# Output projection of a decoder block: 8 x 8 products of tiles, or seven products of quarters

## The chip, the cores and the metric

The kernel runs on one core of one Trainium2 chip. The metric is the device time of one execution in microseconds (us); lower is better. Engines: PE (TensorE, matrix products; PEld is its weight load), DVE (VectorE), ACT (ScalarE), POOL (GpSimd) and SP (SyncE). SP and POOL here mostly issue DMA transfers. Each engine works through its own queue of instructions in a fixed order and waits for semaphores of the others. "Lnnn" is a line of the kernel file.

## The reference

One decoder block, 1024 tokens by 1024 channels, in float32:

```python
y = (sigmoid(gate_sb + b_gate[0]) * (o_sb @ w_branch_sb)        # first branch: stick-breaking attention
     + sigmoid(gate_gla + b_gate[1]) * (o_gla @ w_branch_gla))  # second branch: gated linear attention
h = x + y @ w_out                                               # the output projection
hn = rms_norm(h, norm_ffn_g)
a, g = split(hn @ w_ffn_in)                                     # 1024 -> 2 x 2816
h = h + (gelu(causal_conv(a) + conv_b) * g) @ w_ffn_out
out = rms_norm(h, norm_final_g)
```

The change concerns `y @ w_out` (1024 x 1024 by 1024 x 1024) and the norm behind it.

## The kernel before

Every large product is made in three matmuls: each float32 operand is split into a high half (a rounded copy of type fp32r, a CAST on ACT at L122) and a low half (operand minus high half, on DVE at L113), and high x high + high x low + low x high are summed in one PSUM bank (128 x 512; there are eight). `split`, and the operand makers `piece`, `cut` and `parts` that call it, thus cost one ACT and one DVE instruction of 128 x 512 for each operand.

The functions are generators, and the code steps them against one another; a scheduler then orders the instructions of each engine by what it expects to be ready, and the engines run in that order. SBUF tiles come in three sizes from pools: `t8` (128 x 2048, 16 of them), `t4` (128 x 1024, 14 of them) and `t2` (128 x 512, 11 of them).

- `branch(b, o, w)` projects a branch: for 16 pairs (channel tile, half of the tokens) 12 matmuls, times the gate. The first branch leaves its product in `yb[th, kh]` (token half, channel half; the channels lie on the partitions), the second adds it and splits the sum into `yq`.
- `project()` makes the output projection in four parts (half of the tokens by half of the columns). In a part, each of four token tiles is 8 x 3 matmuls into one bank, then an add of `x`. After the second part of each token half a row is whole: it is stored to `h_d`, normalized (`norm_rows`: square and root on ACT, reciprocal and scaling on DVE) and later turned on PE into the next product's operand: `turn` for tiles 0 to 3; `turn_sums` for tiles 4 to 7, which also makes some of the sums that the next product needs.
- `fast(jobs, hq, EARLY)` is the product with `w_ffn_in`: 22 jobs by Winograd's form of Strassen, with seven products of quarters each. Two of the seven need only the first token half (`hq["11"]`, `hq["12"]`), and the first six jobs make these two early, while the projection ends: 12 steps "early" with 12 matmuls each. With the loading and preparing steps that makes 58 steps in all.
- `phase(first, ...)` begins the last matrix, `w_ffn_out`, in the same form. Its first operands are made ahead: the loop over the remaining job steps counts `n` and, from `n >= AT_END` (51) on, puts `first(0)` into `ready` (L1444, L1445). `weight_sums` makes sums of quarters of `w_ffn_out`, which `pace(3)` steps from `n > FFN_FROM` (18) on.
- The code between: 14 steps of the projection, one job step, two projection steps, two job steps, one projection step; so three job steps are taken ahead of the loop and 55 are left for it.

Of the kernel before, what the change touches and what calls it, by code (L numbers as in the profile page):

```python
# [17 lines left out]
P = 128  # L18
# [39 lines left out]
AT_END = 51  # L58
HEADS_AT = 2
# [9 lines left out]
def block_kernel(ctx: ExitStack, tc: tile.TileContext, x, norm_mix_g, w_in, b_gate, w_alpha_up, b_alpha,  # L69
# [32 lines left out]
    def dram(name, rows, cols, dt=F32):  # L102
        return dp.tile([rows, cols], dt, tag=name, name=name)
# [67 lines left out]
    wsum_d = dram("wsum_d", NH * P, 2 * D)  # L171
# [898 lines left out]
    yq, yb, hq, hs1 = {}, {}, {}, {}  # L1070

    def branch(b, o, w):
# [11 lines left out]
        for n in range(2 * NK):  # L1084
# [27 lines left out]
    def weight_sums():  # L1112

        def rows(k):
            if k < NH:
                v = t4(), t4()
                for i in range(2):
                    nc.sync.dma_start(v[i], w_ffn_out[(i * NH + k) * P:(i * NH + k + 1) * P, :])
                return v

        nxt = rows(0)
        for k in range(NH):
            (a, b), nxt = nxt, rows(k + 1)
# [48 lines left out]

    def project():

        def raws(dh):
            return [load(w_out[k * P:(k + 2) * P, dh * HALF:(dh + 1) * HALF], 2)[:, n]
                    for k in range(0, NK, 2) for n in range(2)]

        parts = [(0, 0), (0, 1), (1, 1), (1, 0)]
        ws = [flat(piece(r)) for r in raws(0)]  # L1180
        late = []

        def late_turn():
# [6 lines left out]
        for part, (th, dh) in enumerate(parts):  # L1190
            c = slice(dh * HALF, (dh + 1) * HALF)
            second, turned = part % 2, part % 2 == 0
            if not second:
                hr = []
                for i in range(4 * th, 4 * th + 4, 2):
                    v = by(t8(F32), 2)
                    nc.sync.dma_start(v, x[i * P:(i + 2) * P, :].rearrange("(n p) c -> p n c", p=P))
                    hr += [v[:, 0], v[:, 1]]
            else:
                for a in ("22", "s3", "s2") if th else ("11", "12"):  # L1200
                    hq[a] = quarter()
            nws = [] if turned else ws
            for n, i in enumerate(range(4 * th, 4 * th + 4)):
                t = slice(n * P, (n + 1) * P)
                pt = bank()
                for k in range(NK):
                    yh, yl = yq[th, k // 4]
                    wh, wl = ws[k]
                    for m, (a, b) in enumerate(((yh, wh), (yl, wh), (yh, wl))):
                        nc.tensor.matmul(pt, a[:, k % 4, t], b, start=(k == 0 and m == 0),  # L1210
                                         stop=(k == NK - 1 and m == 2))
                    if n == 3 and turned:
                        ws[k] = wh = wl = None
                        if k % 2 == 0:
                            raw = load(w_out[k * P:(k + 2) * P, (HALF - dh * HALF):(D - dh * HALF)], 2)
                        nws.append(flat(piece(raw[:, k % 2])))
                h = hr[n]
                add(h[:, c], pt, h[:, c])
                if second:
                    nc.gpsimd.dma_start(h_d[i * P:(i + 1) * P, :], h)  # L1220
                    hn = t4()
                    norm_rows(h, gf, hn)
                    late.append((hn, i))
                if late and (len(late) > 1 if second else n == 1):
                    late_turn()
                yield
            ws = nws
            if second:
                hr = None
                for kh in range(2):  # L1230
                    del yq[th, kh]
# [248 lines left out]
```

## Time and profile before

| | us |
|---|---|
| median of three runs | 1386.93 (1386.27 to 1387.03) |
| the profiled execution, its own time | 1386.67 |
| its span in the trace | 1384.8 |
| granted TensorE clock | 0.997 |
| projection matmuls (L1210), 384 | 88.8 busy |

The span is that of the one profiled execution, from the first to the last instruction; the rest of its time lies around it. In the groups, a row reads: line, engine, operation, tiles, shape, count, then busy us and mean ns of one, then idle time just before with what ended it. An engine that is busy all the time sets the pace, and a wait elsewhere costs nothing by itself.

### The profile page before, as it was taken

How to read it: one execution, taken by the hardware profiler on the slowest of the kernel's cores; microseconds unless marked ns; L12 is line 12 of the kernel's file. 1: busy time of each engine (PE TensorE's matmuls, PEld its weight loads, DVE VectorE, ACT ScalarE, POOL GpSimd, SP SyncE). 2: the span in 40 equal slices, each digit the busy share in tenths (PEclk: the TensorE clock that was granted, in tenths of full speed). 3: DMA queues.
4: the chain of work that ended last, by engine and by line, in shares of the span. 5: the costliest groups of instructions: out<-in, count | busy, mean ns of one | idle time of the engine just before them, and what ended most of it. 6: DMA issues, size and time to landing. Idle time of an engine off the chain costs nothing.

```text
span 1384.8 us, 18329 instructions
## 1 busy us (share of the span) xinstructions
PE 1372.4 (99%) x6559; PEld 1138.8 (82%) x6559; DVE 1064.6 (77%) x1640; ACT 643.9 (46%) x1244; POOL 136.3 (10%) x233
## 2 busy tenths in 40 slices
PE   9999999999999999999999999999999999999997
PEld 6788888888888888888888788888888888888886
DVE  6388688874878877658348998998888977896765
ACT  7334445653766664724126443343333334454654
POOL 2002123101111002200000000000000000000000
PEclk9999999999999999999999999999999999999999
DMA  6335278448776567673325245554444537953332
GB/s 239 132 117 151 84 221 251 143 158 210 216 158 151 131 197 237 198 237 136 136 91 177 52 120 187 196 189 152 150 163 152 182 107 272 322 163 102 99 101 105
DMA packets 164108, 227.92 MB, mean 165 GB/s; under 512 B 10938, under 2 KB 105276, under 8 KB 163506
## 3 DMA queue, kind: packets, MB, share of 16 engines
q1 hardware_dynamic: 134944, 139.01, 33.0%
q0 software_dynamic: 22496, 73.73, 16.8%
q10 hardware_dynamic: 6578, 14.03, 2.7%
q8 instruction: 51, 0.84, 0.3%
q14 instruction: 39, 0.32, 0.1%
HBM read 160.28 MB, written 66.45 MB: 164 GB/s over the span
## 4 chain that ended last, share of the span: by engine, by line
PE 95%; DVE 3%; ACT 1%; issue 0%; DMA 0%; ACTq 0%; DVEq 0%
PE bank L205 58%; PE bank L1343 15%; PE bank L385 6%; PE bank L1210 6%; PE bank L871 3%; PE bank L828 2%; PE bank L842 2%; DVE t L113 2%; PE bank L494 1%; PE bank L340 1%; DVE t L119 1%; PE bank L562 1%; PE bank L1007 1%; PE bank L970 0%; PE bank L994 0%
## 5 line engine op out<-in xcount | busy, mean ns | idle before, releaser
L205 PE MATMUL bank<-t,t 128*128 128x512 f32 x3624 | 861.1, 393 | 0.9 <-DVE t L113 0.7
L205 PEld LDWEIGHTS bank<-t,t 128*128 128x128 f32 x3624 | 676.5, 188 | 143.1 <-DVE t L113 1.6
L113 DVE TENSOR_TENSOR t<-t,t 128x512 fp32r<-128x512 f32 (+3 forms) x655 | 434.6, 697 | 93.5 <-ACT t L122 87.2
L122 ACT CAST t<-t 128x512 fp32r<-128x512 f32 (+1 forms) x543 | 320.3, 627 | 325.4 <-DVE t L113 81.0
L119 DVE TENSOR_TENSOR t<-bank,t 128x512 f32<-128x512 f32 x266 | 179.3, 685 | 97.9 <-PE bank L205 54.9
L1343 PE MATMUL bank<-t,t 128*128 128x512 f32 x924 | 209.6, 389 | 0.0
L1343 PEld LDWEIGHTS bank<-t,t 128*128 128x128 f32 x924 | 173.5, 188 | 36.0
L113 DVE TENSOR_TENSOR t<-bank,t 128x512 fp32r<-128x512 f32 (+4 forms) x124 | 69.5, 574 | 27.5 <-ACT t L122 26.9
L1210 PE MATMUL bank<-t,t 128*128 128x512 f32 x384 | 88.8, 391 | 0.0
L1241 ACT ACTIVATE t<-t,vcol 128x1024 f32<-128x1024 f32 x22 | 27.4, 1245 | 127.5 <-DVE t L119 127.5
L113 DVE TENSOR_TENSOR t<-t 128x512 f32<-128x512 f32 x120 | 83.3, 701 | 4.1 <-DMA t<-in_w_ffn_in_dram 3.7
L1210 PEld LDWEIGHTS bank<-t,t 128*128 128x128 f32 x384 | 71.6, 188 | 14.6
L119 DVE TENSOR_TENSOR t<-t,t 128x512 f32<-128x512 f32 x115 | 75.5, 686 | 9.8 <-ACT t L628 8.6
L122 ACT CAST t<-bank 128x512 fp32r<-128x512 f32 (+3 forms) x120 | 60.3, 512 | 48.8 <-PE bank L842 26.8
L385 PE MATMUL bank<-t,t 128*128 128x512 f32 x336 | 77.9, 391 | 0.0
L385 PEld LDWEIGHTS bank<-t,t 128*128 128x128 f32 x336 | 62.7, 188 | 13.1 <-DVE t L113 0.2
L1243 DVE SCALAR_TENSOR_TENSOR t<-t,vcol,t 128x1023 f32<-128x1023 f32 (+1 forms) x44 | 56.3, 1279 | 14.1 <-ACT t L1241 13.9
L833 DVE TENSOR_TENSOR_SCAN t<-t,t 128x128 f32<-128x128 f32 (+1 forms) x64 | 51.6, 816 | 17.5 <-ACT t L830 17.2
L828 PE MATMUL bank<-t,t 128*128 128x128 f32 (+3 forms) x192 | 54.6, 369 | 0.0
L842 PE MATMUL bank<-ident,t 128*128 128x128 f32 x288 | 53.2, 273 | 0.0
L871 PE MATMUL bank<-t,t 128*128 128x256 f32 (+1 forms) x320 | 51.0, 276 | 1.2 <-ACT t L122 0.7
L830 ACT ACTIVATE t<-bank 128x128 f32<-128x128 f32 (+3 forms) x96 | 46.9, 507 | 7.2 <-DMA osb_d<-t 3.2
(164 smaller groups left out, 813.5 us busy)
## 6 DMA issues: line engine op xcount, KB each, us to landing
t<-in_w_ffn_in_dram SPq DMA_DIRECT2D x50, 512.0 KB, 5.1
t<-in_w_in_dram SPq DMA_DIRECT2D x43, 512.0 KB, 5.3
act_d<-t POOLq DMA_DIRECT2D x22, 512.0 KB, 5.8
t<-in_w_ffn_out_dram SPq DMA_DIRECT2D x22, 512.0 KB, 7.6
wsum_d<-t POOLq DMA_DIRECT2D x22, 512.0 KB, 4.5
t<-act_d SPq DMA_DIRECT2D x22, 512.0 KB, 5.9
t<-wsum_d SPq DMA_DIRECT2D x44, 256.0 KB, 3.1
t<-in_w_ffn_out_dram SPq DMA_DIRECT2D x33, 256.0 KB, 2.7
```

The lines of the kernel that those rows point to most:

```text
L113: nc.vector.tensor_tensor(out=o, in0=a, in1=b, op=ALU.subtract)
L119: nc.vector.tensor_tensor(out=o, in0=a, in1=b, op=ALU.add)
L122: nc.scalar.copy(h, src)
L205: nc.tensor.matmul(pt, a[:, kk], b[:, kk], start=start and kk == 0 and m == 0, stop=stop and kk == k - 1 and m == 2)
L385: nc.tensor.matmul(pt, a[:, k % 4, t], b, start=k == 0 and m == 0, stop=k == NK - 1 and m == 2)
L828: nc.tensor.matmul(z[:, 0:w], q[:, a, e, ts_], kk[:, e, b0 * P:b1 * P], start=a == 0, stop=a == 1)
L833: nc.vector.tensor_tensor_scan(out=kr, data0=kr, data1=above[:, 0:w], initial=1.0, op0=ALU.mult, op1=ALU.max)
L842: nc.tensor.transpose(pt[:, b * P:(b + 1) * P], ke[:, b * P:(b + 1) * P], ident)
L871: nc.tensor.matmul(po[:, c0:2 * P], vt[b][:, head, :], a[b // 4][:, b % 4, c0:], start=(b == 0 and n == 0), stop=(b == nb - 1 and n == 1))
L1210: nc.tensor.matmul(pt, a[:, k % 4, t], b, start=(k == 0 and m == 0), stop=(k == NK - 1 and m == 2))
L1243: nc.vector.scalar_tensor_tensor(out=cv[:, i:], in0=av[:, :S - i], scalar=col(V_CW, (2 - i) * NF + f), in1=cv[:, i:], op0=ALU.mult, op1=AL ...
L1343: nc.tensor.matmul(pts[m][i], a[:, t], b, start=(k == 0 and x_ == 0), stop=(k == NH - 1 and x_ == 2))
```

## The change

The output projection is made as seven products of quarters (512 x 512 by 512 x 512, four k tiles by four token tiles by three matmuls). The second branch no longer splits its sum; it leaves plain sums in `yb`, from which `project` forms the sums of quarters in place. Sums of the quarters of `w_out` are made by `weight_sums`, stepped beside the second branch, and go through a new DRAM tensor `osum_d`. The products run in the order op1, op2, op5, op6, op3, op7, op4 with operands prepared `LEAD` = 2 ahead. Rows of the result are summed into `x` partly by DVE and partly by DMA transfers that accumulate (`onto`, on POOL's queue). op3 ends tile by tile over its last two k tiles, op4 over all four. The norms of tiles 0 to 3 follow op3, those of tiles 4 to 7 follow op4. The table `AMONG` says how many job steps go ahead of each of the last six projection steps: nine in all, so 49 are left for the loop. `AT_END` and `FFN_FROM` stay as they are.

```diff
+LEAD = 2
+AMONG = 1, 0, 1, 1, 3, 3
...
+    wsum_d, osum_d = dram("wsum_d", NH * P, 2 * D), dram("osum_d", 4 * P, 2 * D)
...
             else:
                 mul(sg, pt, sg)
-                add(sg, sg, y)
-                split(*(a[:, i % 4] for a in yq[th, i // 4]), sg)
+                add(y, sg, y)
...
-    wsteps = weight_sums()
+    wsteps = weight_sums(w_ffn_out, NH, wsum_d)
+    osteps = weight_sums(w_out, 4, osum_d)
...
+    def onto(o, a):
+        nc.gpsimd.dma_start(o, a, accum_op=ALU.add)
...
+        def cut(src):
+            v = t4(F32R)
+            v = v[:, :HALF], v[:, HALF:]
+            split(*v, src)
+            return v
...
+        def op1(k):
+            w = weights(w_out, k, 0)
+            a = cut(yb[0, 0][:, k])
+            sub(yb[0, 0][:, k], yb[0, 0][:, k], yb[1, 0][:, k])
+            return a, cut(w)
...
+        def norm(i):
+            nc.gpsimd.dma_start(h_d[i * P:(i + 1) * P, :], hr[i])
+            hn = t4()
+            norm_rows(hr[i], gf, hn)
+            hr[i] = None
+            late.append((step[0], hn, i))
+
+        def done1(i, pt):
+            nc.scalar.copy(c[:, i], pt)
+
+        def done2(i, pt):
+            add(left(i), pt, left(i))
+            onto(left(i), c[:, i])
+
+        def done5(i, pt):
+            nc.scalar.copy(d[:, i], pt)
+            onto(right(i), d[:, i])
+            onto(right(4 + i), d[:, i])
+
+        def done6(i, pt):
+            add(c[:, i], pt, c[:, i])
+            onto(left(4 + i), c[:, i])
+            onto(right(4 + i), c[:, i])
+            add(right(i), right(i), c[:, i])
+
+        def done3(i, pt):
+            add(right(i), pt, right(i))
+            norm(i)
+
+        def done7(i, pt):
+            add(right(4 + i), pt, right(4 + i))
+            add(left(4 + i), pt, left(4 + i))
+
+        def done4(i, pt):
+            sub(left(4 + i), left(4 + i), pt)
+            norm(4 + i)
...
+            if tail:
+                for i in range(4):
+                    for k in range(4 - tail, 4):
+                        rank(k, i)
+                    done(i, pts[i])
+                    step[0] += 1
+                    if late and late[0][0] + 3 <= step[0]:
+                        turn_late()
+                    yield
...
-    for _ in branch(1, og, w_branch_gla):
+    for n, _ in enumerate(branch(1, og, w_branch_gla)):
+        fill(osteps, n % 2)
         pace(1)
...
-    for _ in islice(steps, 14):
-        pace(2)
-    fill(jobs, 1)
-    fill(steps, 2)
-    fill(jobs, 2)
-    fill(steps, 1)
+    fill(steps, 26)
+    for n in AMONG:
+        fill(jobs, n)
+        fill(steps, 1)
+    fill(steps, 16)
```

Lines of the changed file are shifted: the helpers by 2 (L113 becomes L115, L119 L121, L122 L124, L205 L207), the projection's matmul is L1316, `turn_sums`'s transposes L351, the convolution's lines L1353 (ACT), L1355 (DVE) and L1357 (ACT). In the rows below a bracket names what a row waits for: an engine, or a transfer issued on SP or ACT (DMAHW) or on POOL (DMASW).

**First place, PE, the end of the projection.** Before, the transposes of token tile 6 (`t4_1328`) stand behind all 24 matmuls of tile 7 (the last bank is 7067):

```order
L1210 MATMUL bank_1337_7067<-t4_1302_6896,t8_1206_6264 128x512
L1210 MATMUL bank_1337_7067<-t4_1302_6896,t8_1205_6263 128x512
L349 MATMUL bank_1342_7102<-ident_66,t4_1328_7035 128x128 [waits DVE_49]
L349 MATMUL bank_1342_7102<-ident_66,t4_1328_7035 128x128 x3
L349 MATMUL bank_1343_7103<-ident_66,t4_1328_7035 128x128 x4
```

Now op4's banks 7083, 7084 and 7085 are tiles 4, 5 and 6, 7156 is the first early product of job 0, and `t4_1368` is the normalized tile 4:

```order
L1316 MATMUL bank_1358_7083<-t4_1367_7100,t4_1366_7097 128x512 [waits DVE_49]
L1316 MATMUL bank_1358_7083<-t4_1367_7100,t4_1366_7097 128x512
L1316 MATMUL bank_1359_7084<-t4_1367_7100,t4_1366_7097 128x512 x2
L207 MATMUL bank_1380_7156<-t8_1324_6908,t4_1356_7077 128x512
L207 MATMUL bank_1380_7156<-t8_1323_6907,t4_1356_7077 128x512
L1316 MATMUL bank_1360_7085<-t4_1364_7092,t4_1363_7089 128x512 x2
L1316 MATMUL bank_1360_7085<-t4_1367_7100,t4_1366_7097 128x512 x3
L351 MATMUL bank_1391_7198<-ident_66,t4_1368_7117 128x128 [waits DVE_49]
L351 MATMUL bank_1391_7198<-ident_66,t4_1368_7117 128x128 x3
```

Between tile 4's last matmul and its transposes stand nine matmuls.

**Second place, DVE, ahead of the first full job.** `t4_1392` (before) and `t4_1450` (now) are the low half of that job's first piece. Before:

```order
L113 TENSOR_TENSOR t2_1390_7395<-t8_1389_7392 128x512 [waits DMAHW2_49,DMAHW1_49]
L119 TENSOR_TENSOR t4_1383_7334<-bank_1385_7349,t4_1383_7334 128x512 [waits PE_49,Activation_49]
L113 TENSOR_TENSOR t2_1391_7396<-t8_1389_7392,t2_1390_7395 128x512 [waits DVE_49]
L113 TENSOR_TENSOR t2_1393_7402<-t8_1389_7392 128x512
L113 TENSOR_TENSOR t2_1394_7403<-t8_1389_7392,t2_1391_7396 128x512 [waits DVE_49]
L113 TENSOR_TENSOR t2_1405_7466<-t8_1398_7415 128x512 [waits DMAHW5_49,DMAHW3_49]
L113 TENSOR_TENSOR t2_1406_7467<-t8_1398_7415,t2_1405_7466 128x512 [waits DVE_49]
L113 TENSOR_TENSOR t4_1392_7399<-t2_1391_7396,t4_1392_7399 128x512 [waits Activation_49]
```

Now (`t8_1440`, `t8_1442` and `t2_1433` belong to the sums of `last_sums`; bank 7515 is the last early product):

```order
L115 TENSOR_TENSOR t8_1442_7467<-t2_1405_7270,t8_1441_7466 128x4x128 [waits Activation_49]
L115 TENSOR_TENSOR t8_1442_7467<-t2_1421_7354,t8_1441_7466 128x4x128 [waits Activation_49]
L121 TENSOR_TENSOR t4_1444_7494<-bank_1446_7515,t4_1444_7494 128x512 [waits PE_49]
L115 TENSOR_TENSOR t2_1433_7429<-t8_1325_6909,t2_1432_7428 128x512 [waits DVE_49]
L115 TENSOR_TENSOR t2_1448_7538<-t8_1447_7535 128x512 [waits DMAHW7_49,DMAHW6_49]
L121 TENSOR_TENSOR t2_1433_7429<-t2_1433_7429,t8_1326_6910 128x512 [waits DVE_49]
L115 TENSOR_TENSOR t2_1449_7539<-t8_1447_7535,t2_1448_7538 128x512 [waits DVE_49]
L115 TENSOR_TENSOR t2_1451_7545<-t8_1447_7535 128x512
L115 TENSOR_TENSOR t8_1442_7467<-t2_1433_7429,t8_1441_7466 128x4x128 [waits Activation_49]
L115 TENSOR_TENSOR t4_1450_7542<-t2_1449_7539,t4_1450_7542 128x512 [waits Activation_49]
```

The last sums of `last_sums` and the last early add now stand directly ahead of that low half, and it stands 127 rows behind op6's first add.

**Third place, ACT, the start of the last matrix.** `t4_1868` to `t4_1871` (before) and `t4_1959` to `t4_1962` (now) are the first two operand pairs of `phase(first, ...)`; L1241 (now L1353) opens a job's convolution. Before, ahead of job 20's convolution:

```order
L122 CAST t4_1868_10228<-t8_1865_10222 128x512 [waits DMAHW4_49,DMAHW7_49,DMASW5_49,DMASW1_49]
L122 CAST t4_1869_10231<-t2_1866_10224 128x512 [waits DMAHW6_49]
L122 CAST t4_1870_10235<-t8_1865_10222 128x512 [waits DMASW0_49,DVE_49]
L122 CAST t4_1871_10238<-t2_1867_10226 128x512 [waits DMAHW7_49,PE_49]
L122 CAST t4_1877_10287<-t2_1875_10284 128x512 [waits PE_49]
L122 CAST t4_1878_10291<-t2_1876_10285 128x512 [waits DMASW3_49]
L122 CAST t4_1879_10294<-t2_1862_10211 128x512 [waits PE_49]
L1241 ACTIVATE t4_1880_10297<-t4_1852_10143,vcol_75 128x1024 [waits DVE_49]
```

Now, behind the opening of the last job's (21's) convolution:

```order
L1353 ACTIVATE t4_1944_10526<-t4_1932_10416,vcol_75 128x1024 [waits DVE_49]
L124 CAST t4_1959_10560<-t8_1956_10554 128x512 [waits DMAHW6_49]
L124 CAST t4_1960_10563<-t2_1957_10556 128x512 [waits DMAHW3_49]
L1357 ACTIVATE t4_1944_10526<-t4_1944_10526 128x1024 [waits DVE_49,Activation_49]
L124 CAST t4_1959_10560<-t2_1972_10644 128x512 [waits DMAHW1_49,DVE_49,PE_49]
L124 CAST t4_1961_10579<-t8_1956_10554 128x512 [waits DVE_49]
L124 CAST t4_1962_10582<-t2_1958_10558 128x512 [waits DMAHW4_49]
```

The first pair moved behind job 21's opening, and a later cast that reuses `t4_1959` moved ahead of the second pair. On DVE the first pair's low halves stand behind both convolution steps (L1355) of job 21.

More of the change, by code (lines that the diff above doesn't have):

```diff
@@ L1190, in project @@
[L1190 to L1231, printed above, removed]
@@ new lines, in op2, with op5, op6 @@
+        def op2(k):
+            w = weights(w_out, 4 + k, 0)
+            return cut(yb[0, 1][:, k]), cut(w)
+        def op5(k):
+            w = weights(osum_d, k, 1)
+            s1 = yb[1, 0][:, k]
+            add(s1, s1, yb[1, 1][:, k])
+            return cut(s1), cut(w)
+        def op6(k):
+            w = weights(osum_d, k, 0)
+            s2 = yb[1, 0][:, k]
+            sub(s2, yb[1, 1][:, k], yb[0, 0][:, k])
+            a = cut(s2)
+            s4 = yb[0, 1][:, k]
+            sub(s4, s4, s2)
+            if k == 3:
+                del yb[1, 0]
+            return a, cut(w)
@@ new lines, in left, with right @@
+        def left(i):
+            return hr[i][:, :HALF]
+        def right(i):
+            return hr[i][:, HALF:]
+        def norm(i):
[9 more added lines that the diff above has]
+            onto(left(i), c[:, i])
@@ new lines, in done4, with turn_late, prepare @@
+        def done4(i, pt):
+            sub(left(4 + i), left(4 + i), pt)
+            norm(4 + i)
+        late, step, hr = deque(), [0], []
+        def turn_late():
+            _, hn, i = late.popleft()
+            if i in (0, 4):
+                for a in ("22", "s3", "s2") if i else ("11", "12"):
+                    hq[a] = quarter()
+            if i < 4:
+                turn(hn, i, hq)
+            else:
+                turn_sums(hn, i, hq, hs1)
+        operands = []
+        def prepare(n):
+            while len(operands) < min(n, 28):
+                p, k = divmod(len(operands), 4)
+                operands.append(PROD[p][0](k))
@@ new lines, in project, with rank @@
+        PROD = ((op1, done1, 0), (op2, done2, 0), (op5, done5, 0), (op6, done6, 0), (op3, done3, 2), (op7, done7, 0),
+                (op4, done4, 4))
+        prepare(1 + LEAD)
+        for i in range(0, NT, 2):
+            v = by(t8(F32), 2)
+            nc.sync.dma_start(v, x[i * P:(i + 2) * P, :].rearrange("(n p) c -> p n c", p=P))
+            hr += [v[:, 0], v[:, 1]]
+        v = None
+        c, d = (by(t8(F32), 4) for _ in range(2))
+        for p, (_, done, tail) in enumerate(PROD):
+            pts = [bank() for _ in range(4)]
+            def rank(k, i):
+                (ah, al), (bh, bl) = operands[4 * p + k]
+                t = slice(i * P, (i + 1) * P)
+                for m, (a, b) in enumerate(((ah, bh), (ah, bl), (al, bh))):
+                    nc.tensor.matmul(pts[i], a[:, t], b, start=(k == 0 and m == 0), stop=(k == 3 and m == 2))
+            for k in range(4):
+                prepare(4 * p + k + 1 + (LEAD if p < 6 else 0))
+                if k < 4 - tail:
+                    for i in range(4):
+                        rank(k, i)
+                        if k == 3:
+                            done(i, pts[i])
+                    operands[4 * p + k] = None
+                    step[0] += 1
[3 more added lines that the diff above has]
+            if tail:
+                for i in range(4):
+                    for k in range(4 - tail, 4):
+                        rank(k, i)
+                    done(i, pts[i])
+                    step[0] += 1
+                    if late and late[0][0] + 3 <= step[0]:
+                        turn_late()
+                    yield
+                for k in range(4 - tail, 4):
+                    operands[4 * p + k] = None
+            if p == 4:
+                c = d = None
@@ L1236, in ff_cols @@
+        while late:
+            turn_late()
+            yield
     def ff_cols(f):
```

52 lines of the change are left out of this document (29 added, 23 removed).

## The prediction

> **What bounds the kernel now.** I read the page first, then the order of time of TensorE (PE), then stretches of the stage that changes, then VectorE (DVE) in order of time. From the page, the span, PE's share and the chain that ended last:
>
> ```profile
> span 1384.8 us, 18329 instructions
> PE 1372.4 (99%) x6559; PEld 1138.8 (82%) x6559; DVE 1064.6 (77%) x1640; ACT 643.9 (46%) x1244; POOL 136.3 (10%) x233
> PE 95%; DVE 3%; ACT 1%; issue 0%; DMA 0%; ACTq 0%; DVEq 0%
> ```
>
> PE is busy 99% and is 95% of the chain. So every matmul taken away is worth its pitch, and every time PE waits for an operand is lost for good. PE in order of time from the output projection on (start, duration, line, count, idle before):
>
> ```profile
> 653.12 32.81 PE L1210 MATMUL bank<-t,t 128*128 128x512 f32 x144
> 685.76 1.03 PE L340 MATMUL bank<-ident,t 128*128 128x128 f32 x8
> 686.55 5.70 PE L1210 MATMUL bank<-t,t 128*128 128x512 f32 x24
> 692.10 1.03 PE L340 MATMUL bank<-ident,t 128*128 128x128 f32 x8
> ...
> 771.63 128.59 PE L205 MATMUL bank<-t,t 128*128 128x512 f32 x566 [0.74 <-DVE t L113]
> ```
>
> The first 144 matmuls take 685.76 - 653.12 = 32.64 us, 0.2267 us each. A row of 24 with its eight transposes takes 692.10 - 685.76 = 6.34 us, so the transposes cost 6.34 - 24 x 0.2267 = 0.90. PE waits once between 653 and 900, 0.74 us, for a low half made at L113. Who has room there? Four stretches (stretch, its length, then busy us and count of PE, PEld, DVE, ACT, POOL, granted clock, DMA share, GB/s): the end of the gated branch, the second branch projection, the output projection, and the early products after it:
>
> ```profile
> 560.00:600.00 40.00, 39.99 (x270) 32.94 (x271) 22.13 (x44) 30.93 (x126) 5.20 (x10) 1.00 0.59 190
> 608.00:653.00 45.00, 45.00 (x200) 37.27 (x199) 35.23 (x55) 14.76 (x25) 0.00 (x0) 1.00 0.58 203
> 653.00:745.80 92.80, 92.80 (x437) 77.30 (x436) 45.29 (x69) 28.00 (x55) 3.80 (x7) 1.00 0.31 110
> 745.80:790.00 44.20, 43.35 (x196) 35.03 (x195) 42.72 (x72) 24.41 (x45) 0.53 (x1) 1.00 0.47 126
> ```
>
> DVE is half idle in the projection (45.29 of 92.80) and full right behind it (42.72 of 44.20). The change puts DVE work into the first and takes PE time from under the second. DVE's own pitch, from its order of time:
>
> ```profile
> 735.78 0.15 DVE L328 RECIPROCAL ri<-rs 128x1 f32<-128x1 f32 x1
> 735.85 0.67 DVE L113 TENSOR_TENSOR t<-t,t 128x512 fp32r<-128x512 f32 x1
> 736.44 1.28 DVE L332 SCALAR_TENSOR_TENSOR t<-t,ri,t 128x1024 f32<-128x1024 f32 x1
> 737.64 0.68 DVE L113 TENSOR_TENSOR t<-t,t 128x512 fp32r<-128x512 f32 x1
> ...
> 763.67 2.50 DVE L113 TENSOR_TENSOR t<-t,t 128x512 fp32r<-128x512 f32 x4
> 766.08 0.69 DVE L119 TENSOR_TENSOR t<-t,t 128x512 f32<-128x512 f32 x1
> ```
>
> Back to back, four 512-wide operations take 766.08 - 763.67 = 2.41, 0.60 each although one lasts 0.69; a 1024-wide norm takes 737.64 - 736.44 = 1.20; a reciprocal 0.07.
>
> **The change part by part.** The sum is made against the profiled execution's own 1386.67 us (its span and 1.87 around it); the median of the three runs is 0.26 above it.
>
> (a) Matmuls. 8 x 8 x 2 x 3 = 384 become 7 x 4 x 4 x 3 = 336: 48 x 0.2267 = -10.9. Transposes and early products stay as many, only in another place. The wait of 0.74 at 771.63 goes with its order: -0.7.
>
> (b) DVE behind the sixth product's first finished row. Call the first matmul of the projection 0. Until then nothing is short: six products give PE 6 x 10.88 us less the last, and DVE prepares operands up to five pairs ahead, as far as the 1024-wide tiles reach. The fourth product in order (op6) finishes its first row at 3 x 10.88 + 3 x 2.72 + 0.68 = 41.5. From there to the low half that the first full job needs (second piece of order in the chapter on the change) DVE has 128 rows: 112 of 512 (67.2 us), 8 norms (9.6) and 8 reciprocals (0.8), together 77.6. PE has 2.0 left of op6, 3 x 48 + 144 early matmuls (288 x 0.2267 = 65.3), eight groups of transposes (7.2) and two matmuls that need high halves alone (0.5): 75.0. Before, the projection's matmuls were PE time under which DVE had little to do; now the last three products and the early ones carry nearly all DVE work of the stage, and DVE is the longer of the two. It also idles in there, since both queues run in order: eight adds and two low halves after op6 last 6.0, so DVE stands 2.7 until op3's first row at 43.5 + 5.44 + 1.36 = 50.3; 1.1 around that norm's chain; and 1.9 at row 4. How long a norm's chain is:
>
> ```profile
> 680.52 0.69 DVE L119 TENSOR_TENSOR t<-bank,t 128x512 f32<-128x512 f32 x1 [2.81 <-PE bank L1210]
> 682.75 0.16 DVE L328 RECIPROCAL ri<-rs 128x1 f32<-128x1 f32 x1 [1.54 <-ACT rs L327]
> 682.95 1.28 DVE L332 SCALAR_TENSOR_TENSOR t<-t,ri,t 128x1024 f32<-128x1024 f32 x1
> ```
>
> From the add to a turnable row are 682.95 + 1.28 - 680.52 = 3.7 us. Before, a whole row of 24 matmuls (5.4) lay between; in the first piece of order, nine matmuls (2.0) lie between row 4's last one and its transposes, and ACT squares two rows ahead of the first root, so the chain is about 5: a wait of about 3 at that place. The rest shows as about 1 at row 1's transposes and about 5 at the first full job. Total: 77.6 + 5.7 idle + 0.7 for dependent pairs - 75.0 = **+9.0**. Bounds: DVE never idle, 77.6 - 75.0 = 2.6; with 5 us more idling at the other norms, 13 to 14. I take 9.0 because the idle times follow from the order itself. 16 low halves and 16 casts leave the second branch; DVE there has 45.00 - 35.23 = 9.8 to spare, so that buys nothing.
>
> How sure is 0.60? "VectorE: DVE Perf Modes" of the Trainium skill (section "The DRAIN you can't avoid") says that the next operation does not start until the pipe is empty; read so, each of the 112 rows would cost its whole 0.69 and the sum would be 10 us more. The trace disagrees for these forms: rows start 0.60 apart while one lasts 0.69.
>
> (c) The start of the last matrix. The preparing of its first operands is tied to step 51 of the remaining job steps. Before, 55 steps remained after three; now nine are taken among the projection, 49 remain, and step 51 never comes. The third piece of order shows it: the first two pairs were cast ahead of job 20's convolution, now they stand behind job 21's. In the trace of before (PE; ACT; DVE), around the end of the last job:
>
> ```profile
> 1139.64 28.50 PE L205 MATMUL bank<-t,t 128*128 128x512 f32 x125
> 1167.97 17.39 PE L1343 MATMUL bank<-t,t 128*128 128x512 f32 x76
> ...
> 1144.71 2.71 ACT L122 CAST t<-t 128x512 fp32r<-128x512 f32 x5 [3.65 <-DVE t L113]
> ...
> 1166.18 1.25 ACT L1241 ACTIVATE t<-t,vcol 128x1024 f32<-128x1024 f32 x1 [11.96 <-DVE t L119]
> 1167.33 1.12 ACT L122 CAST t<-t 128x512 fp32r<-128x512 f32 x2
> 1170.63 1.06 ACT L1245 ACTIVATE t<-t 128x1024 f32<-128x1024 f32 x1 [2.18 <-DVE t L1243]
> ...
> 1169.26 1.27 DVE L1243 SCALAR_TENSOR_TENSOR t<-t,vcol,t 128x1022 f32<-128x1022 f32 x1
> 1170.46 1.29 DVE L113 TENSOR_TENSOR t<-t,t 128x512 fp32r<-128x512 f32 x2
> ```
>
> Job 21 ends on PE at 1167.97. The two casts and two low halves that stand there now become the first pair: casts done at 1168.45 (PE waits 0.5, then four matmuls on high halves, 0.9), low halves done at 1171.75 (waits 2.4), eight matmuls to 1173.6. ACT's next cast reuses the first pair's tile, so it waits for those; then come two casts at 0.55 for the second pair: 1175.3 (waits 1.7). Sum **+4.6**; at least 2.9 (the low halves alone), at most 6 with a late load. Nothing else covers it.
>
> (d) Weight sums. Sixteen DVE rows (9.6 us) go into the end of the gated branch, where DVE is busy 22.13 of 40.00; eight loads and eight stores of 512 KB are new on SP and POOL there. Rows of such transfers (KB each, us to landing), with those for (e):
>
> ```profile
> t<-in_w_out_dram SPq DMA_DIRECT2D x16, 512.0 KB, 4.3
> wsum_d<-t POOLq DMA_DIRECT2D x22, 512.0 KB, 4.5
> dv_d<-t POOLq DMA_DIRECT2D x9, 256.0 KB, 2.4
> t<-sqkl_d POOLq DMA_DIRECT2D x24, 256.0 KB, 6.7
> t<-gv_d POOLq DMA_DIRECT2D x2, 1024.0 KB, 9.0
> L1220 POOL DMA_DIRECT2D h_d<-t x7 | 3.8, 542 | 150.5 <-DVE t L119 150.5
> ```
>
> A DVE row that waits for a load holds up the reciprocals behind it, and with them the branch's norm. In four such places a late load could cost up to 0.8 each: 0 to 3, I take +0.5, since DVE idles there nearly half the time.
>
> (e) Row sums by DMA: 20 accumulating transfers of 256 KB on POOL's queue, 0.54 each to issue. The eight of the third product are issued from 31.4 to 35.5; the first DVE row that waits for them is the add of op6 at 42 to 45. No row of before accumulates. Nearest: 2.4 (a 256 KB store), 6.7 (a load), 9.0 (four times the bytes): all inside the 10 us of room, so 0; the other end is a rival.
>
> Sum: -10.9 - 0.7 + 9.0 + 4.6 + 0.5 = +2.5, that is 1389.2, and 1389.4 as a median.
>
> **Rivals.**
> - DVE keeps up. If the DVE rows do not idle (2.6), the start costs 2.9 and (d) nothing, it is -11.6 + 5.5 = -6.1: 1380.8. For it: PE waited 0.74 in all with DVE full. Against it: the order puts the adds, norms and operands in one queue behind op3. It decides when the wait at the first full job is under 1 us.
> - The accumulating DMAs come late. If one takes twice a load, 13.4, the adds of op6 wait 3; if the eight run one behind the other at 2.4 they end at 31.4 + 19 = 50.6, 5 to 6 late; at 3.5 each, 59, 14 late. Every us is PE's, since DVE is the longer queue: 1392 to 1403, say 1396. Decisive from about 11 us to landing on.
> - DVE at 0.69 a row, by the rule above: 1399. The rows against it are quoted; 3 in 100.
>
> That the change does not do what it says is excluded by the order: 336 matmuls stand there.
>
> **How the numbers follow.** Forecast, 1386 to 1393: 0.50. DVE keeps up wholly or in part, 1379 to 1386: 0.24. DMAs late: 0.16. Rule: 0.03. Other waits, either way: 0.07. About 0.2% (2.8 us) is what a measurement of this kernel tells from no change: 1384.1 and 1389.7. The forecast's range lies about half below 1389.7 (0.23 same, 0.27 slower). Faster: 0.17 + 0.03 = 0.20; same 0.23 + 0.07 + 0.03 = 0.33; slower 0.27 + 0.16 + 0.03 + 0.01 = 0.47. The range of 8 in 10 is 1381 to 1397, the sums of the lower ends (-6.1) and of the upper (-11.6 + 13 + 6 + 3 = +10.4).
>
> **What would show it.** Of the changed kernel: 336 projection matmuls at 0.227 without a wait in the first four products; PE waiting for DVE near row 4's transposes (about 3) and at the first full job (about 5); DVE without a gap from row 4 to there; PE waiting 4 to 5 in two or three pieces at the start of the last matrix; the adds behind op6 not waiting for a DMA. I am wrong if those waits are missing, or if DVE waits for the accumulating DMAs.

## The result and the profile after

The changed kernel takes 1403.15 us (median of four runs, 1402.03 to 1407.38) against 1386.95 us; the ratio is 1.0124, with a 95% interval of 1.0102 to 1.0145. So it is 16 us slower, where 1389.4 was forecast and 1381 to 1397 was the range. The profiled execution took 1402.59 us, 15.9 more than that of before. The top of its page (span; busy time and share of PE, PEld, DVE, ACT and POOL):

```profile
span 1400.3 us, 18470 instructions
PE 1371.2 (98%) x6511; PEld 1134.1 (81%) x6511; DVE 1101.4 (79%) x1700; ACT 656.2 (47%) x1268; POOL 159.3 (11%) x261
```

PE has 48 matmuls fewer and yet is busy only 1.2 us less than before, so its matmuls are slower somewhere; and it waits more. Who PE waits for (us in total, times, longest), the waits that before has too left out:

```profile
PE bank L207 <- ACT t L124: 5.6, 2, 4.8
PE bank L1044 <- ACT t L1038: 3.5, 2, 2.8
PE bank L351 <- DVE t L334: 2.7, 1, 2.7
PE bank L1455 <- DVE t L115: 2.1, 1, 2.1
PE bank L1455 <- ACT t L124: 1.7, 2, 1.3
...
PE bank L1009 <- POOL t L1001: 1.4, 1, 1.4
...
PE bank L342 <- DVE t L334: 0.5, 1, 0.5
...
PE bank L207 <- DVE t L115: 0.4, 1, 0.4
```

PE in order of time, the rows at which a stage begins or a wait stands (L1316 is the projection, L1455 the last matrix, L1044 and L1009 belong to the gated branch):

```profile
578.46 1.10 PE L1044 MATMUL bank<-ident,t 128*128 128x128 f32 x4 [2.80 <-ACT t L1038]
590.80 1.10 PE L1044 MATMUL bank<-ident,t 128*128 128x128 f32 x4 [0.66 <-ACT t L1038]
593.27 1.23 PE L1009 MATMUL bank<-t,t 128*128 128x128 f32 x8 [1.36 <-POOL t L1001]
594.18 2.88 PE L207 MATMUL bank<-t,t 128*128 128x512 f32 x6
...
660.72 54.34 PE L1316 MATMUL bank<-t,t 128*128 128x512 f32 x239
...
744.32 1.92 PE L351 MATMUL bank<-ident,t 128*128 128x128 f32 x8 [2.73 <-DVE t L334]
...
788.89 388.19 PE L207 MATMUL bank<-t,t 128*128 128x512 f32 x1704 [4.81 <-ACT t L124]
1177.45 1.21 PE L1455 MATMUL bank<-t,t 128*128 128x512 f32 x4 [0.37 <-ACT t L124]
1180.74 3.31 PE L1455 MATMUL bank<-t,t 128*128 128x512 f32 x8 [2.07 <-DVE t L115]
1185.37 207.04 PE L1455 MATMUL bank<-t,t 128*128 128x512 f32 x912 [1.32 <-ACT t L124]
```

Against before, where the projection began at 653.12 and the last matrix at 1167.97, that splits the 15.5 us of span into three:

| stretch | before | after | difference | forecast |
|---|---|---|---|---|
| up to the projection | 653.1 | 660.7 | +7.6 | +0.5 (d) |
| projection and 22 jobs (to 1177.08, where the next wait begins) | 514.9 | 516.4 | +1.5 | -11.6 + 9.0 = -2.6 (a, b) |
| last matrix and end | 216.8 | 223.2 | +6.4 | +4.6 (c) |

The first line, the weight sums, is the largest miss. Of its 7.6 us, 2.80 + 0.66 + 1.36 = 4.8 are PE's waits between 575 and 594; most of the rest is slower matmuls behind them (the six at 594.18 took 2.88, where six took 1.64 before). The other lines show the next miss: in the second stretch PE's waits sum to 0.53 + 2.73 + 0.76 + 0.35 + 4.81 = 9.2, nearly the 9.0 of the forecast, yet the stretch is 4.1 us longer than forecast. The granted clock tells why (stretch, its length, then busy us and count of PE, PEld, DVE, ACT, POOL, the clock, DMA share, GB/s), behind the waits of the gated branch and around the two long waits of the second stretch:

```profile
578.50:585.00 6.50, 6.50 (x40) 5.16 (x42) 4.38 (x8) 3.37 (x11) 2.25 (x4) 1.00 0.80 281
595.00:600.00 5.00, 5.00 (x23) 4.08 (x22) 4.42 (x7) 2.60 (x7) 1.07 (x2) 0.74 0.83 313
...
741.60:744.30 2.70, 0.00 (x0) 0.00 (x0) 2.17 (x4) 1.84 (x5) 0.64 (x2) 1.00 0.96 373
744.30:748.00 3.70, 3.68 (x13) 3.27 (x14) 2.99 (x5) 0.96 (x2) 0.00 (x0) 0.54 0.38 153
748.00:752.00 4.00, 4.00 (x19) 3.27 (x18) 2.67 (x5) 2.40 (x6) 0.00 (x0) 1.00 0.06 11
784.00:788.90 4.90, 0.09 (x2) 0.01 (x1) 4.90 (x9) 1.30 (x3) 0.00 (x0) 0.99 0.00 0
788.90:792.00 3.10, 3.10 (x7) 2.11 (x8) 3.06 (x6) 1.31 (x3) 0.00 (x0) 0.50 0.00 0
792.00:796.00 4.00, 4.00 (x19) 3.30 (x18) 4.00 (x8) 1.88 (x4) 0.00 (x0) 0.97 0.07 18
```

After PE has stood still for 2.7 and for 4.8 us, its clock is 0.54 and 0.50 for some 3.5 us, and half of that time is lost on top of the wait. Each of these two waits thus costs almost 2 us more than its length. The length of a wait alone does not decide this: behind the wait of 2.80 us at 578.46 the clock is 1.00, and behind the two short ones at 590.80 and 593.27 it is 0.74.

### The profile page after: what moved, and what is told of

Its sections match the earlier page's. It is cut to its first block, busy times and chain, and to the rows that moved or that the text cites. A ratio compares the mean times of both kernels' runs of the same rounds, so it can differ in the third digit from the quotient of the medians.

```text
span 1400.3 us, 18470 instructions
## 1 busy us (share of the span) xinstructions
PE 1371.2 (98%) x6511; PEld 1134.1 (81%) x6511; DVE 1101.4 (79%) x1700; ACT 656.2 (47%) x1268; POOL 159.3 (11%) x261
## 4 chain that ended last, share of the span: by engine, by line
PE 93%; DVE 3%; ACT 1%; issue 1%; DMA 1%; POOL 0%; ACTq 0%; DVEq 0%; POOLq 0%
PE bank L207 57%; PE bank L1455 15%; PE bank L387 5%; PE bank L1316 5%; PE bank L873 2%; PE bank L830 2%; PE bank L844 2%; DVE t L115 1%; DVE t L121 1%; PE bank L342 1%; PE bank L564 1%; PE bank L496 1%; PE bank L972 0%; DMA t<-in_w_out_dram 0%; DVE t L334 0%
## 5 line engine op out<-in xcount | busy, mean ns | idle before, releaser
L207 PE MATMUL bank<-t,t 128*128 128x512 f32 x3624 | 865.9, 394 | 5.9 <-ACT t L124 5.6
L207 PEld LDWEIGHTS bank<-t,t 128*128 128x128 f32 x3624 | 678.7, 189 | 149.2 <-ACT t L124 6.4
L115 DVE TENSOR_TENSOR t<-t,t 128x512 fp32r<-128x512 f32 (+3 forms) x691 | 456.5, 695 | 106.8 <-ACT t L124 98.1
L124 ACT CAST t<-t 128x512 fp32r<-128x512 f32 (+1 forms) x559 | 327.9, 626 | 317.0 <-DVE t L115 65.6
L121 DVE TENSOR_TENSOR t<-bank,t 128x512 f32<-128x512 f32 x270 | 180.8, 683 | 72.3 <-PE bank L207 63.5
L1455 PE MATMUL bank<-t,t 128*128 128x512 f32 x924 | 211.6, 391 | 3.8 <-DVE t L115 2.1
L1455 PEld LDWEIGHTS bank<-t,t 128*128 128x128 f32 x924 | 173.9, 188 | 41.5 <-ACT t L124 2.8
L1353 ACT ACTIVATE t<-t,vcol 128x1024 f32<-128x1024 f32 x22 | 27.4, 1245 | 146.4 <-DVE t L121 146.4
L121 DVE TENSOR_TENSOR t<-t,t 128x512 f32<-128x512 f32 x127 | 83.3, 684 | 9.6 <-ACT t L630 8.6
L115 DVE TENSOR_TENSOR t<-t 128x512 f32<-128x512 f32 x124 | 85.4, 695 | 4.6 <-DMA t<-in_w_ffn_in_dram 4.1
L115 DVE TENSOR_TENSOR t<-bank,t 128x512 fp32r<-128x512 f32 (+4 forms) x124 | 69.2, 572 | 24.0 <-ACT t L124 23.6
L1316 PE MATMUL bank<-t,t 128*128 128x512 f32 x336 | 78.1, 390 | 0.0
L124 ACT CAST t<-bank 128x512 fp32r<-128x512 f32 (+3 forms) x120 | 60.2, 513 | 32.2 <-PE bank L844 27.8
L1316 PEld LDWEIGHTS bank<-t,t 128*128 128x128 f32 x336 | 62.9, 188 | 12.9
L1355 DVE SCALAR_TENSOR_TENSOR t<-t,vcol,t 128x1023 f32<-128x1023 f32 (+1 forms) x44 | 56.2, 1278 | 15.0 <-ACT t L1353 14.9
L1359 POOL DMA_DIRECT2D act_d<-t x22 | 11.7, 532 | 351.1 <-DVE t L118 351.1
## 6 DMA issues: line engine op xcount, KB each, us to landing
t<-in_w_ffn_in_dram SPq DMA_DIRECT2D x50, 512.0 KB, 4.9
t<-in_w_in_dram SPq DMA_DIRECT2D x43, 512.0 KB, 5.5
act_d<-t POOLq DMA_DIRECT2D x22, 512.0 KB, 5.6
t<-in_w_ffn_out_dram SPq DMA_DIRECT2D x22, 512.0 KB, 7.8
wsum_d<-t POOLq DMA_DIRECT2D x22, 512.0 KB, 3.6
t<-act_d SPq DMA_DIRECT2D x22, 512.0 KB, 6.4
```

The lines of the kernel that those rows point to most:

```text
L115: nc.vector.tensor_tensor(out=o, in0=a, in1=b, op=ALU.subtract)
L121: nc.vector.tensor_tensor(out=o, in0=a, in1=b, op=ALU.add)
L124: nc.scalar.copy(h, src)
L207: nc.tensor.matmul(pt, a[:, kk], b[:, kk], start=start and kk == 0 and m == 0, stop=stop and kk == k - 1 and m == 2)
L1316: nc.tensor.matmul(pts[i], a[:, t], b, start=(k == 0 and m == 0), stop=(k == 3 and m == 2))
L1355: nc.vector.scalar_tensor_tensor(out=cv[:, i:], in0=av[:, :S - i], scalar=col(V_CW, (2 - i) * NF + f), in1=cv[:, i:], op0=ALU.mult, op1=AL ...
```

## The experiments

All times are medians beside runs of the kernel before on the same chip (1386.8 there each time).

**The job loop's tables.** The edit on the changed kernel:

```diff
-FFN_FROM = 18
+FFN_FROM = 12
-AT_END = 51
+AT_END = 45
```

> The changed kernel with the two tables of the job loop brought back to its length (AT_END 45 for 51, FFN_FROM 12 for 18), so that the last matrix's first operands are made ahead again. Theory A (the lost preparing costs its three waits, 0.4 + 2.1 + 1.3 = 3.8 us, and as much again in the matmuls behind them at the lower granted clock, 5.7 us in all between the last job and the last matmul): 1403.2 - 5.7 = 1397.4, no wait of TensorE at the start of the last matrix, its 924 matmuls in 209.6 as before. Rival B (the waits alone count, the slower matmuls have another cause): 1399.4, and the 924 matmuls still take over 211.

Measured: 1395.58, ratio 1.0066 (1.0051 to 1.0081). From its groups, the matmuls of the last matrix, with no idle time:

```profile
L1455 PE MATMUL bank<-t,t 128*128 128x512 f32 x924 | 209.6, 389 | 0.0
```

No wait is left there and the 924 matmuls take 209.6 as before: theory A by its signs, 1.8 us faster than its time. The lost preparing is worth 7.6 us by the medians, of which its waits are 3.8; the four runs on either side spread over 4.4 and 5.4 us, so 7.6 is a rough figure. The two tables were changed together, and no run parts them.

**The weight sums, alone and elsewhere.** First, the kernel before with the sums and nothing else of the change:

```diff
-    for _ in branch(1, og, w_branch_gla):
+    for n, _ in enumerate(branch(1, og, w_branch_gla)):
+        fill(osteps, n % 2)
         pace(1)
+    fill(osteps, 16)
```

> The kernel before, with the sums of w_out made and stored beside the second branch exactly where the changed kernel makes them; nothing reads them. Theory A (the sums' rows stand in VectorE's queue between the gated branch's norms and wait for their loads, so the norms come late): the whole 7.6 us by which the changed kernel's projection starts later, 1394.5, with TensorE waiting some 5 us in all for the scaled rows of the norms between 570 and 600. Rival B (the stretch is longer because the second branch and the operands behind it were rewritten): within 1 us of the kernel before, 1387 to 1388.

Measured: 1396.08, ratio 1.0059 (1.0042 to 1.0077): 9.3 us for sums that nobody reads. The projection begins at 664.15. Then the changed kernel with the sums later:

```diff
-        fill(osteps, n % 2)
+        fill(osteps, (n >= 22) * 2)
```

> The changed kernel with the sums of w_out stepped from the 23rd step of the second branch on, two steps at a time, so that in VectorE's queue all their rows stand behind the last norm of the gated branch. Theory A (it is their place, not their number): projection starts at 653 to 654 as before, total 1403.2 - 7 = 1396, if the sums are stored in time for the third product; a store that comes too late would show as a wait of the third product's operands. Rival B (the eight loads and stores compete with the branch's own loads wherever they stand): 1400 or more, projection starts at 657 or later.

Measured: 1397.13, ratio 1.0073 (1.0057 to 1.0088). PE's first row of the projection stands where it stood before the change:

```profile
652.92 54.34 PE L1316 MATMUL bank<-t,t 128*128 128x512 f32 x239
```

So both runs say that it is the sums, and their place. Which part of them? Two more on the kernel before: loads and stores without the VectorE rows, then loads and rows without the stores (in both the eight loads remain).

```diff
+            if nh > 4:          # for w_out: no sums
                 sub(b22, b22, b12)
                 sub(b12, b12, b11)
             yield
+            if nh > 4:
                 add(b11, b22, b11)
                 sub(b21, b11, b21)
```

> The kernel before with the eight loads and eight stores of the sums of w_out, but without their 16 VectorE rows (the weights are stored as they were loaded, and nothing reads them). Theory A (VectorE's rows that wait for the loads hold up the norms' reciprocals): the delay of 11 us in the kernel with all of the sums goes, 1387 to 1389. Rival B (the sums hold 128x1024 tiles until their stores land, and the second branch's weights wait for one of them in SyncE's queue; ScalarE's casts then wait for those weights, and the norms' squares stand behind the casts): a good half of the delay stays, 1391 to 1395, and ScalarE waits over 3 us for the second branch's weights near 585.

```diff
-            for i, v in enumerate((a, b)):
+            for i, v in enumerate((a, b) if nh > 4 else ()):
```

> The kernel before with the eight loads and 16 VectorE rows of the sums of w_out, without their eight stores. Theory A (the stores are what costs: they hold the 128x1024 tiles for some 5 us more, so that SyncE's load of the second branch's weights waits, and GpSimd's selects stand behind them): most of the delay of 11 us goes, 1387 to 1390. Rival B (VectorE's rows that wait for loads cost as much by themselves, since norms' reciprocals stand behind them): 1391 to 1397.

Measured: 1393.94 without the rows (1.0051, 1.0035 to 1.0066), 1391.07 without the stores (1.0030, 1.0018 to 1.0042). So 7.1 stay without the rows and 4.3 without the stores, where all of it costs 9.3: by the times rival B in both, in the second at the very edge of its range. No run has the loads alone, so what they cost by themselves is not known. Theory A of sums_no_dve (the reciprocals in VectorE's queue are all of it) fell, and with it the picture that I had from the first run. The changed kernel's own trace has the places. VectorE, SyncE's queue, its longest wait for a store, and ScalarE, each in order of time:

```profile
577.22 0.69 DVE L115 TENSOR_TENSOR t<-t,t 128x512 f32<-128x512 f32 x1 [0.96 <-DMA t<-in_w_out_dram]
577.83 0.17 DVE L1035 RECIPROCAL ss<-ss 128x4 f32<-128x4 f32 x1
...
581.09 0.38 SPq L183 DMA_DIRECT2D t<-in_w_branch_gla_dram  x1
...
SPq L183 <- DMA osum_d<-t: 7.1, 1, 7.1
...
586.96 1.66 ACT L124 CAST t<-t 128x512 fp32r<-128x512 f32 x3 [5.08 <-DMA t<-in_w_branch_gla_dram]
588.52 0.27 ACT L1033 ACTIVATE t<-bank 128x128 f32<-128x128 f32 x1
```

and SyncE's queue in the trace of before:

```profile
563.84 0.38 SPq L181 DMA_DIRECT2D t<-in_w_branch_gla_dram  x1
```

The reciprocal of a norm (L1035) stands behind a row that waits for its weights; that ends in PE's wait of 2.80 at 578.46. And the second of the four loads of the second branch's weights, at 563.84 before, goes out at 581.09: its 128 x 1024 tile comes from the pool that the sums use too, and SyncE waits 7.1 us until a store of theirs has landed. ScalarE's casts wait 5.08 for that load, and the next norm's squares (L1033) stand behind the casts. In GpSimd's queue the gated branch's selects stand behind the stores, which wait for loads or rows. This shows without any of the rows, in sums_no_dve (POOL, then PE):

```profile
579.60 0.53 POOL L1134 DMA_DIRECT2D osum_d<-t  x1 [2.31 <-DMA t<-in_w_out_dram]
580.13 1.23 POOL L999 TENSOR_SCALAR_AFFINE_SELECT t<-t 128x512 f32<-128x512 f32 x2
...
580.84 1.57 PE L1007 MATMUL bank<-t,t 128*128 128x128 f32 x8 [2.74 <-POOL t L999]
596.38 2.07 PE L1007 MATMUL bank<-t,t 128*128 128x128 f32 x8 [4.29 <-POOL t L999]
```

Rival B of sums_no_dve had named another place, ScalarE waiting over 3 us for the second branch's weights near 585. SyncE does wait there for a store to land, 5.4 us, but ScalarE waits only 2.41 for the weights, at 596; PE's two long waits are those for GpSimd. In sums_no_store it is the reciprocal behind a row (DVE, then PE):

```profile
577.41 0.69 DVE L113 TENSOR_TENSOR t<-t,t 128x512 f32<-128x512 f32 x1 [2.60 <-DMA t<-in_w_out_dram]
578.02 0.17 DVE L1033 RECIPROCAL ss<-ss 128x4 f32<-128x4 f32 x1
...
578.65 1.22 PE L1042 MATMUL bank<-ident,t 128*128 128x128 f32 x4 [3.25 <-ACT t L1036]
```

**The accumulating DMAs.** `onto` issues nothing:

```diff
-        nc.gpsimd.dma_start(o, a, accum_op=ALU.add)
+        pass
```

> The changed kernel with all 20 accumulating DMAs left out, so a part of the row sums is missing from its output. Theory A (they land well before the adds that need them, and nothing waits for them): within 1 us of the changed kernel, 1402 to 1404. Rival B (they slow VectorE or the loads by contention, or an add waits for them): 1 to 6 us faster, 1397 to 1402.

Measured: 1400.48, ratio 1.0099 (1.0084 to 1.0114). By the number that is rival B's band; by the trace it is not its mechanism. The waits of the projection are the same to 0.1 us. The profiled run is 3.4 us shorter in two places that do not wait for these DMAs: the projection begins 1.9 earlier, before the first of them is issued, and behind the wait at row 4 the clock stays full in this run:

```profile
742.49 1.09 PE L351 MATMUL bank<-ident,t 128*128 128x128 f32 x8 [2.73 <-DVE t L334]
```

The same eight transposes behind the same wait of 2.73 took 1.92 in the changed kernel. The intervals of the two ratios overlap as well. I count the DMAs as free in the projection; a small cost elsewhere is not excluded.

**Both places mended.** The edits of at_end and sums_late22 together.

> The changed kernel with both of the edits tried alone before: the job loop's tables fit its length, and the sums of w_out stand behind the gated branch's norms. Theory A (two separate places): their gains add up, 1403.2 - 7.6 - 6.0 = 1389.6, and what is left over the kernel before are the waits of the projection (0.5 + 2.7 + 1.1 + 4.8 = 9.1 us) with the slower matmuls behind the two long ones (1 to 2 us each at least) against 11.6 saved. Rival B (one hides a part of the other): 1392 or more.

Measured: 1390.03, ratio 1.0023 (1.0015 to 1.0032); the gains add up. What is left is term (b) with its slow clock, and a new wait of 1.9 for an early job's weights.

**What sets the wait at the first full job?** The changed kernel without the low halves of the operands of op7 and op4:

```diff
+        def high(src):
+            v = t4(F32R)[:, :HALF]
+            nc.scalar.copy(v, src)
+            return v, v
...
-            a = cut(yb[1, 1][:, k])
+            a = high(yb[1, 1][:, k])
...
-            return a, cut(w)
+            return a, high(w)
```

> The changed kernel with the low halves of the operands of op7 and op4 left out (the high half is used in their place, so its output is less exact): 16 rows of 0.60 us fewer on VectorE, as many matmuls. Theory A (the wait at the first full job is VectorE's volume): that wait and the 1.1 us just ahead of it go, the 2.7 us at row 4's transposes stay, since those are the length of a norm's chain and no volume: 1403.2 - 5.9 = 1397, or 1395 with the slower matmuls behind the wait gone too. Rival B (a chain of dependent rows from the last norm to the first job's operands sets the wait): more than 3 us of it stay, 1400 or more.

Measured: 1400.13, ratio 1.0089 (1.0075 to 1.0103): rival B by its number, and the opposite of theory A in its places. The wait at row 4 and the 1.1 are gone, the one at the first full job stays (PE in order of time):

```profile
786.51 389.38 PE L207 MATMUL bank<-t,t 128*128 128x512 f32 x1704 [5.33 <-ACT t L124]
```

The rows left out were ahead of op4's first finished row. Leaving them out did not shorten the wait at the first full job; it took away the smaller waits ahead of it, so the stretch from the projection to the last matrix is 512.0 us for 516.4. The order of PE differs there too: row 4's transposes begin 7.3 us behind VectorE's row 4, in the changed kernel 4.7, so this run does not say how much of the gain is volume and how much is cover.

From VectorE's row 4 to its low half for the first full job are 49 us in both traces (737.33 to 786.31, and 739.60 to 788.66). From the norm of row 4 on it idles only 0.6 us there, and 2.2 in the changed kernel: so it is no chain but a full queue, and it is the work behind that point that PE's cover must match.

Next, the transposes of rows 4 to 7 a step later, on both_fixed:

```diff
-AMONG = 1, 0, 1, 1, 3, 3
+AMONG = 1, 0, 1, 1, 2, 2, 2
...
-                    if late and late[0][0] + 3 <= step[0]:
+                    if late and late[0][0] + 3 + (p > 4) <= step[0]:
```

> both_fixed, with the transposes of rows 4 to 7 one projection step later and the job steps beside them dealt 1, 0, 1, 1, 2, 2, 2. Theory A (the wait of 2.7 us at row 4's transposes is a chain that lacks cover, and is saved when cover is put there): 2.7 us faster than both_fixed, some 4 with the slower matmuls behind it, 1386 to 1387. Rival B (VectorE is the longer queue from the sixth product to the first full job, so the wait only moves): the wait at the first full job grows by as much, within 1 us of both_fixed.

Measured: 1387.31, ratio 1.0002 (0.9993 to 1.0011), no difference from before. The row of PE behind the wait, and the clock in the two stretches behind it:

```profile
779.88 389.64 PE L207 MATMUL bank<-t,t 128*128 128x512 f32 x1704 [7.99 <-ACT t L124]
...
779.90:783.00 3.10, 3.10 (x7) 2.11 (x8) 3.10 (x6) 1.31 (x3) 0.00 (x0) 0.50 0.00 0
783.00:786.00 3.00, 3.00 (x9) 2.32 (x8) 2.96 (x6) 2.46 (x5) 0.00 (x0) 0.50 0.00 0
```

Rival B in the waits: 2.73 + 1.10 at three places became 3.18 more at one. Theory A in the time: 2.7 faster than both_fixed. In the profiled executions the stretch from the projection to the last matrix is 4.2 us shorter; 1.6 of that are waits (11.4 against 9.8), and most of the rest fits the clock, which is near half behind three waits of both_fixed (1.87, 2.73 and 4.81) and behind only one, though for 6 us, here. So, more cover behind that point: one and two early jobs more, on row4a.

```diff
-EARLY = 6
+EARLY = 7       # and 8
```

with AT_END 47 and 49, FFN_FROM 14 and 16.

> row4a with EARLY 7 for 6: one job more makes its two early products ahead of the first full job (24 matmuls, 5.44 us of TensorE, with three VectorE rows, 1.8 us), and the job loop's tables fitted to it. Theory A (from the last product's first finished row to the first full job VectorE is the longer queue, so TensorE's cover counts): the wait of 8.0 at the first full job shrinks by 5.44 - 1.8 = 3.6, and the kernel with it: 1387.3 - 3.6 = 1383.7. Rival B (the wait is a chain of dependent rows behind the early jobs, or the 128x1024 tile that one more early result holds delays the operands): the wait stays, 1386 to 1390.

Measured: 1386.54, ratio 0.9999 (0.9990 to 1.0009), in rival B's range. The wait fell from 8.0 to 5.9 only, and another of 2.65 stands at 872.04; why one job more helps so little stays open.

> row4a with EARLY 8. Theory A: the wait at the first full job falls by 7.2 to under 1 us, and the slower matmuls behind it go too: 1387.3 - 7.2 - 2 = 1378. Rival B: as with 7, 1386 to 1390, or worse, since two more tiles are held.

Measured: **1379.56**, ratio 0.9949 (0.9934 to 0.9964), 7.3 us faster than the kernel before. PE from the projection on:

```profile
653.81 54.34 PE L1316 MATMUL bank<-t,t 128*128 128x512 f32 x239
...
779.03 4.85 PE L207 MATMUL bank<-t,t 128*128 128x512 f32 x20 [1.76 <-DVE t L115]
784.08 376.00 PE L207 MATMUL bank<-t,t 128*128 128x512 f32 x1656 [0.19 <-ACT t L124]
1159.91 209.60 PE L1455 MATMUL bank<-t,t 128*128 128x512 f32 x924
```

Projection and jobs now take 1159.91 - 653.81 = 506.1 against 514.9 before: 8.8 us less, and 11.2 with the waits of 0.5 + 1.8 + 0.2 added, near the 11.6 that the seven products were to save. Is that the early jobs' own gain? The kernel before with EARLY 8 (AT_END 55, FFN_FROM 22):

> The kernel before with EARLY 8 for 6 and the job loop's tables fitted. It waits 0.74 at its first full job. Theory A (the cover is worth something only where VectorE is the longer queue, so the gain of 8 early jobs belongs to the seven products): at most 0.7 us, 1386.1 to 1387. Rival B (eight early jobs are better in themselves): 1380 to 1385.

Measured: 1386.81, ratio 1.0000 (0.9991 to 1.0010): no. Eight early jobs are worth something only beside the seven products.

**GpSimd in VectorE's place**, on row4a:

```diff
-        first_pieces(nxt)
-        more_pieces(nxt)
+        first_pieces(nxt, ppiece, psub)      # differences and low halves by nc.gpsimd
+        more_pieces(nxt, ppiece, psub)
```

> row4a with the first full job's four differences and four low halves made on GpSimd instead of VectorE (128x512; the trace of before has such rows on GpSimd at 1.29 us each). Theory A (volume behind the last product's first row): eight rows of 0.60 fewer, the wait of 8.0 falls to 3.2, 1387.3 - 4.8 = 1382.5. Rival B (on GpSimd they take 8 x 1.29 = 10.3 us and slow VectorE's rows beside them): the wait stays above 6, 1386 or more.

Measured: 1395.63, ratio 1.0064 (1.0049 to 1.0079), 8.3 slower than row4a: rival B. On GpSimd (first row: two low halves) and PE:

```profile
780.86 3.97 POOL L243 TENSOR_TENSOR t<-t,t 128x512 fp32r<-128x512 f32 x2 [6.00 <-ACT t L248]
...
780.84 1.22 PE L207 MATMUL bank<-t,t 128*128 128x512 f32 x2 [6.87 <-ACT t L248]
783.19 73.70 PE L207 MATMUL bank<-t,t 128*128 128x512 f32 x312 [1.14 <-POOL t L243]
859.20 317.02 PE L207 MATMUL bank<-t,t 128*128 128x512 f32 x1390 [2.30 <-DVE t L115]
```

The first two low halves take 2.0 each there, the other two 1.5 and the differences 1.3 to 1.7, and the low halves lie in the chain to the matmul. VectorE's rows beside them are slower too: four of 128x512 take 3.55 at 780.14, where four took 2.50 in the trace of before. With EARLY 7 as well:

> Both: EARLY 7 and the first full job's eight rows on GpSimd. Theory A: the wait of 8.0 falls by 3.6 + 4.8, to nothing, and the slower matmuls behind it go: 1387.3 - 8 - 2 = 1377. Rival B: no better than the better one of the two alone.

Measured: 1392.11, ratio 1.0036 (1.0023 to 1.0049). Rival B: worse than EARLY 7 alone.

## Why the prediction was wrong

- (a) held: 336 matmuls at the same pitch, and the best version shows 11.2 of the 11.6 us.
- (b) held in its waits, 9.2 for 9.0, and in its places: 2.7 for 3 at row 4's transposes, 0.5 for 1 at row 1's, and 4.8 for 5 at the first full job; two short waits, 1.1 together, were not foreseen. The agreement of the sums is in part luck. VectorE came to the end of the low half that the first full job needs 128.5 us after the first matmul, where the sum has 125.5, and idled 8.0 us on the way for 5.7; PE's matmuls were longer as well, behind row 4's wait. (In the sum, eight reciprocals at 0.07 are 0.6, not 0.8.) And the balance was drawn from the wrong point for the longest wait. It counted VectorE's 128 rows from op6's first row on; less_dve shows that 16 rows left out ahead of op4's first row do not shorten the wait at the first full job, and that the work behind that row decides it.
- (c) held in its waits, 3.8 for 4.6, and was too small in its price: 5.7 between the last job and the last matmul, 7.6 by the medians of at_end.
- (e) held. The eight DMAs of the third product were issued from 692.80 to 699.7, that is 32.1 to 39.0 after the first matmul, and the add of op6 at 702.98 waits for none; all twenty land after 3.4 to 10.6 us, 6.8 in the middle. Only the issuing took longer than the 0.54 each of the forecast.
- **The step that failed is (d)**: "In four such places a late load could cost up to 0.8 each: 0 to 3, I take +0.5, since DVE idles there nearly half the time." It measured 7.6 in the trace, 9.3 alone on the kernel before. It looked at one queue, VectorE's, and at rows. The sums also take tiles from a pool that the second branch's loads use, and stand in GpSimd's and SyncE's queues ahead of that branch's own work. Mean idle time said nothing: what counts is who stands behind the row that waits.
- **The second mis-sized term is the price of a wait.** Every wait was counted at its length. Behind those of 2.73 and 4.81, and behind that of 2.07 at the last matrix, the matmuls ran at about half the clock: in the projection and the jobs the stretch is some 4 us longer than its waits explain, at the last matrix 2.0 (5.7 less the waits of 3.8).
- Together: 7.1 missed in (d), 4.1 in the second stretch (0.2 of it waits), 1.8 in the third (0.8 less in waits, the rest clock and 0.7 behind the last matmul, which no run explains): 13.0, the difference between +2.5 and +15.5.

Of the rivals none came: VectorE did not keep up, and the DMAs were not late. For the rival at 0.69 a row, the waits of (b) would have had to be 10 us longer.

## What to carry to other kernels

Before new work is put into a stretch with idle engines, list for each queue that it enters, and for each pool that it takes tiles from, what stands behind it: a row, a store or a load that waits holds all of that up. When a stage is two queues in a race, draw the balance from the last point at which the longer one waited for the other; rows saved ahead of that point did not shorten the wait behind it here. Where an edit changes the number of steps of a loop, look for the numbers elsewhere that count those steps.

## What the runs showed of the hardware

A wait of PE can be dearer than its length. Behind every wait of 3.0 us or more in these traces the clock fell to 0.50 within 4 us, and behind those of 4.8 to 8.0 it was 0.50 for 3 to 6 us. Between 1.3 and 2.9 us both occur: it fell to about half behind 1.36 us in before_sums (at 576.97) and 1.87 in both_fixed, and stayed at 1.00 behind 2.80 in the changed kernel and 2.83 in less_dve; behind the same wait of 2.73 us it was 0.54 in the changed kernel and 1.00 in no_onto. "TensorE: Matmul & The Clock Gate" of the Trainium skill (section "What's actually happening") has a half-rate state after about 3.4 us without work, judged by a window that runs freely; that would explain why one and the same wait is punished in one run and not in the next, and why the four runs of the changed kernel spread over 5.4 us and those of before over 0.8; no run here tests that. As a limit for a harmless gap the 3.4 us do not hold here: 2.73 us of idle PE were enough in the changed kernel, and 1.36 in before_sums.

Issuing an accumulating DMA kept GpSimd busy 0.83 to 3.2 us, 1.8 in the middle, where the store of a finished row beside it took 0.53 to 0.56.
